# Moving the row loads of VectorE's modulation sums from SyncE's queue to GpSimd's

## The chip, the cores and the metric

The kernel runs on one core of a Trainium2 chip. Its time is the device time of one execution in microseconds (us), and a kernel's time is the median over its runs. The engines are TensorE (PE, matmuls), VectorE (DVE), ScalarE (ACT), GpSimd (POOL) and SyncE (SP). Each works through its own list of instructions in order. A transfer (DMA) is an instruction on the list of the engine that issues it: here SP for most loads, POOL for some stores and loads. An instruction that has to wait holds up all that stand behind it on its engine.

## The reference, cut to what matters

One decoder layer on 512 tokens of width 2048, in float32. A vector `mod` of 6 x 2048 numbers, computed from the conditioning vector `c`, shifts, scales and gates the two halves of the layer.

```python
mod = jax.nn.silu(c) @ w_ada + b_ada
sh1, sc1, gt1, sh2, sc2, gt2 = jnp.split(mod, 6, axis=-1)
h = rms_norm(x, g_pre_mix) * (1.0 + sc1) + sh1
proj = h @ w_in                       # q, k, v, gates, RG-LRU branches
mix = concat(rms_norm(o_att), rms_norm(o_rnn)) @ w_out
x = x + gt1 * rms_norm(mix, g_post_mix)
h = rms_norm(x, g_pre_mlp) * (1.0 + sc2) + sh2
f = jnp.square(jax.nn.relu(h @ w_ff1)) @ w_ff2
x = x + gt2 * rms_norm(f, g_post_mlp)
```

Four of the six parts of `mod` (gt1, sh2, sc2, gt2; numbers 2, 3, 4 and 5 in the code) are computed in the way that the change touches.

## The kernel before, in words

Matmuls run in about float32 accuracy from split operands: a raw weight is copied by ScalarE into a high part and VectorE subtracts that from the raw weight to get the low part, and three matmuls use the pairs. So each weight costs a load, a ScalarE instruction and a VectorE instruction ("the split", lines 102 and 103) before PE can use it. In the first half of the program weights go through two raw buffers `wr` (loaded in line 84, by SP) into slots `sl`. In the two MLP products raw weights `fr` (line 1294, by SP, three buffers) are summed in pairs (`fs`, lines 1315 to 1318) and split into `fh` and `fl` (lines 1299 and 1300), as a Strassen-like scheme with seven products instead of eight wants.

The four modulation parts are not computed on PE but on VectorE, as dot products. `w_ada` is stored transposed, so that a partition holds one output and the free axis the 2048 inputs. `qdot` loads a piece `md` of 128 outputs x 512 inputs (256 KB, line 217) and multiplies it in one VectorE instruction (line 218, "a dot" below) with the row `ca`, which holds 512 values of silu(c) copied to all partitions (line 216, 256 KB), while the products are summed along the free axis into a column of `dq`. Each part takes 64 dots, 256 in all; after every 16 dots `ca` is loaded anew for the next quarter of the inputs. `ca` has one buffer, so its load waits for the last dot with the old one. `md` goes round in a ring of buffers, and a load waits for the dot that used its buffer: six buffers during attention, six shared with other temporaries (`tmp`) during the output projection, and two in the second MLP product.

The program runs in stages: the first projection; attention and RG-LRU with the rest of the input projection (about 217 to 660 us), with 112 dots; the output projection with `wout` (about 660 to 845 us), with 80 dots; the first MLP product; the second (from about 1500 us), with 64 dots from 1478 us on, one at each of its first steps. The output projection goes over four blocks (0 to 3) of 512 columns and 16 pieces of the inner dimension. In blocks 0 to 2, each weight piece serves four row blocks at once; in block 3 the row blocks go one after the other, so that the first of them needs all 16 pieces within a short time. A block is evacuated in line 1072.

The code is written in one order, but a scheduler sets the order in which each engine's list is built, from its own picture of when things are ready; so a change of one queue can move instructions on all engines. POOL's list before holds the stores of the two halves' outputs (`oat`, line 793, and `orn`, line 850), of `ud` (the first MLP product's results, lines 1148, 1421 and 1423) and the loads of `ud` back into `uf` (line 1434), each of which waits for the VectorE work that makes its data or frees its buffer.

Of the kernel before, what the change touches and what calls it, by code (L numbers as in the profile page):

```python
# [13 lines left out]
S = 512  # L14
# [116 lines left out]
def hybrid_block_kernel(ctx: ExitStack, tc: tile.TileContext, xT, c, vec, wada, wst, win, wv0, wv1,  # L131
                        w1, w2, pe, wrg, wout, wff1, wff2, xN, out):
    nc = tc.nc
    V, A, T, G = nc.vector, nc.scalar, nc.tensor, nc.gpsimd
# [73 lines left out]
    def qdot(pool, s_, n, ring=("md", NMD)):  # L208
        for _ in range(min(n, len(QD[s_]))):
            k, q_ = QD[s_].pop(0)  # L210
            w = pool.tile([128, S], F32, name="md", tag=ring[0], bufs=ring[1])
            if k == 0 or CA["pool"] is not pool:
                CA["pool"] = pool
                ca = CA[0] = pool.tile([128, S], F32, name="ca", tag="ca", bufs=1)
                row = cad[0, S * q_:S * q_ + S]
                nc.sync.dma_start(ca, bass.AP(tensor=row.tensor, offset=row.offset, ap=[[0, 128], [1, S]]))
            nc.sync.dma_start(w, wada[s_, k, :, S * q_:S * q_ + S])
            (V.scalar_tensor_tensor(w, w, 0.5, CA[0], op0=OP.mult, op1=OP.mult,  # L218
                                                            accum_out=dq[s_][:, q_, k:k + 1]))

# [726 lines left out]
    def attention(pair, natoms):  # L947
# [10 lines left out]
        for s_ in range(-1, n + TD + 2):  # L958
# [31 lines left out]
            while nmod[0] >= 1:  # L990
                qdot(bp, 2 if QD[2] else 4 if QD[4] else 3, 1)
                nmod[0] -= 1
# [7 lines left out]
    fill(n2 - n1)  # L1000
    attention(1, n3 - n2)
    qdot(bp, 2, 64)
    qvec(gg1, 2, V_GQM)

# [116 lines left out]
    def cdots(x):  # L1121
        nd_[0] += x * nd_[1]
        while nd_[0] >= 1:
            nd_[0] -= 1
            qdot(mp, 4 if QD[4] else 3, 1, ("tmp", NTMP))
# [414 lines left out]
    for s, (kind, q, g) in enumerate(GR):  # L1540
        if kind == "f":
            k, n = q
# [184 lines left out]
```

## Time and profile before

| what | value |
|---|---|
| median of 3 runs | 2205.11 us (2202.41 to 2206.97) |
| profiled execution | 2201.8 us, its span 2200.1 us |
| PE busy | 2095.3 us |
| VectorE busy | 1880.2 us |
| ScalarE busy | 1392.3 us |
| GpSimd busy, its DMA issues counted | 63.7 us |
| VectorE idle just before a dot, waiting for `md` / for `ca` | 34.9 us / 18.5 us |

The span is the time from the first to the last instruction of one profiled execution; the rest of its time lies around it. Busy times are those of the instructions on an engine. A wait is put down to the instruction or transfer that came last before the waiting instruction went on.

### The profile page before, as it was taken

Reading aid. Unit: us, or ns where it says so; the run is one execution under the profiler, and the core shown is the slowest. Engines: PE = TensorE matmul, PEld = TensorE weight load, DVE = VectorE, ACT = ScalarE, POOL = GpSimd, SP = SyncE. Lnnn points to the kernel's source line nnn. Section 1 sums busy time; section 2 is a strip of 40 time slices with the busy share of each in tenths; the row PEclk is TensorE's granted clock in tenths of the full one; section 3 lists DMA queues with packets and bytes.
Section 4 is the critical chain, followed back from the end, with each engine's and each line's share of the span. In section 5 each row is a group of like instructions: output and inputs, shape, how many; then the busy total and the mean of one; then the engine's idle time right before and its main releaser. Section 6 shows DMA issues by size and latency. Waiting matters only on the chain.

```text
span 2200.1 us, 39399 instructions
## 1 busy us (share of the span) xinstructions
PE 2095.3 (95%) x14621; PEld 1915.6 (87%) x14621; DVE 1880.2 (85%) x3762; ACT 1392.3 (63%) x2536; POOL 63.7 (3%) x119
## 2 busy tenths in 40 slices
PE   7998999999999989899999999998999999999995
PEld 3687777878877867899999999998999999999995
DVE  8987999877887777879999999999998887887788
ACT  4349889548994327765555555545766677767764
POOL 0000000000000000000000000000000000000010
PEclk8999999999999999999999999999999999999998
DMA  9764554662126885555555555566766544444453
GB/s 367 310 241 136 191 166 148 219 196 67 59 94 226 285 292 186 192 172 173 186 180 171 176 187 178 192 206 206 253 219 207 190 162 142 165 150 158 138 171 116
DMA packets 138818, 411.12 MB, mean 187 GB/s; under 512 B 18225, under 2 KB 25281, under 8 KB 134273
## 3 DMA queue, kind: packets, MB, share of 16 engines
q1 hardware_dynamic: 126178, 341.49, 46.3%
q0 software_dynamic: 12448, 67.12, 8.8%
q8 instruction: 115, 1.88, 0.3%
q14 instruction: 77, 0.63, 0.1%
HBM read 366.58 MB, written 41.97 MB: 186 GB/s over the span
## 4 chain that ended last, share of the span: by engine, by line
PE 63%; DVE 17%; ACT 8%; DMA 8%; issue 4%; SPq 0%; DVEq 0%; ACTq 0%; POOLq 0%; POOL 0%
DMA md<-wada 4%; PE ps_pj L1132 3%; PE ps_pj L1133 3%; PE ps_pj L1134 3%; DVE fl L1300 3%; PE ps_pj L1479 3%; PE ps_pj L1480 3%; PE ps_pj L1481 3%; DVE md L218 2%; PE ps_S L1134 2%; PE ps_S L1132 2%; PE ps_T L1132 2%; PE ps_S L1133 2%; PE ps_T L1133 2%; PE ps_T L1134 2%
## 5 line engine op out<-in xcount | busy, mean ns | idle before, releaser
L1299 ACT ACTIVATE fh<-fs 128x1024 fp32r<-128x1024 f32 x256 | 273.0, 1066 | 326.2 <-DVE fs L1318 120.9
L1300 DVE TENSOR_TENSOR fl<-fs,fh 128x1024 fp32r<-128x1024 f32 x256 | 312.6, 1221 | 97.1 <-ACT fh L1299 94.6
L1299 ACT ACTIVATE fh<-fr 128x768 fp32r<-128x768 f32 (+2 forms) x296 | 217.1, 735 | 71.5 <-PE ps_pj L1133 11.7
L1300 DVE TENSOR_TENSOR fl<-fr,fh 128x768 fp32r<-128x768 f32 (+2 forms) x296 | 241.1, 816 | 19.1 <-ACT fh L1299 19.0
L102 ACT ACTIVATE sl<-wr 128x512 fp32r<-128x512 f32 (+2 forms) x252 | 145.6, 606 | 146.5 <-DMA wr<-wout 85.2
L218 DVE SCALAR_TENSOR_TENSOR md<-md,ca 128x512 f32<-128x512 f32 x256 | 171.8, 687 | 57.2 <-DMA md<-wada 34.9
L103 DVE TENSOR_TENSOR sl<-wr,sl 128x512 fp32r<-128x512 f32 (+2 forms) x252 | 163.8, 664 | 49.2 <-ACT sl L102 35.9
L1315 DVE TENSOR_TENSOR fs<-fr 128x512 f32<-128x512 f32 x256 | 175.5, 686 | 5.6 <-DMA fr<-wff 3.9
L1479 PE MATMUL ps_pj<-fh,AH 128*128 128x256 f32 x602 | 168.9, 281 | 0.6 <-ACT ps_pj L1459 0.3
L1480 PE MATMUL ps_pj<-fl,AH 128*128 128x256 f32 x602 | 169.0, 281 | 0.0
L1481 PE MATMUL ps_pj<-fh,AL 128*128 128x256 f32 x602 | 168.7, 280 | 0.0
L177 PE MATMUL ps_pj<-AH,sl 128*128 128x512 f32 x384 | 162.2, 422 | 0.4 <-ACT tr L818 0.4
L179 PE MATMUL ps_pj<-AH,sl 128*128 128x512 f32 x384 | 153.5, 400 | 1.5 <-DVE sl L103 1.5
L178 PE MATMUL ps_pj<-AL,sl 128*128 128x512 f32 x384 | 153.5, 400 | 0.0
L1479 PEld LDWEIGHTS ps_pj<-fh,AH 128*128 128x128 f32 x602 | 113.8, 189 | 1.6 <-ACT ps_pj L1459 1.6
L1480 PEld LDWEIGHTS ps_pj<-fl,AH 128*128 128x128 f32 x602 | 113.9, 189 | 0.3 <-DVE fl L1300 0.3
L1481 PEld LDWEIGHTS ps_pj<-fh,AL 128*128 128x128 f32 x602 | 114.0, 189 | 0.0
L1480 PE MATMUL ps_S<-fl,AH 128*128 128x256 f32 x394 | 110.4, 280 | 1.4 <-DVE fl L1300 1.4
L1479 PE MATMUL ps_S<-fh,AH 128*128 128x256 f32 x394 | 110.4, 280 | 1.3 <-ACT ps_S L1459 1.2
L1481 PE MATMUL ps_T<-fh,AL 128*128 128x256 f32 x396 | 110.8, 280 | 0.0
L1479 PE MATMUL ps_T<-fh,AH 128*128 128x256 f32 x396 | 110.8, 280 | 0.0
L1318 DVE TENSOR_TENSOR fs<-fs,fr 128x256 f32<-128x256 f32 x256 | 107.8, 421 | 3.5
(630 smaller groups left out, 7292.7 us busy)
## 6 DMA issues: line engine op xcount, KB each, us to landing
fr<-wff SPq DMA_DIRECT2D x276, 512.0 KB, 3.7
md<-wada SPq DMA_DIRECT2D x256, 256.0 KB, 4.3
uf<-ud POOLq DMA_DIRECT2D x32, 896.0 KB, 4.8
wr<-win SPq DMA_DIRECT2D x48, 512.0 KB, 3.7
ada<-wada SPq DMA_DIRECT2D x22, 1024.0 KB, 10.6
wr<-wout SPq DMA_DIRECT2D x36, 512.0 KB, 4.9
ud<-uf POOLq DMA_DIRECT2D x18, 896.0 KB, 5.3
ud<-uf POOLq DMA_DIRECT2D x14, 768.0 KB, 4.9
```

The lines of the kernel that those rows point to most:

```text
L103: self.nc.vector.tensor_sub(lo, raw, self.f(hi))
L177: T.matmul(o, wh, mh, start=start, stop=False)
L218: (V.scalar_tensor_tensor(w, w, 0.5, CA[0], op0=OP.mult, op1=OP.mult, accum_out=dq[s_][:, q_, k:k + 1]))
L1132: T.matmul(o, wh, b[0], start=start, stop=False, skip_group_check=True)
L1133: T.matmul(o, wh, b[1], start=False, stop=False, skip_group_check=True)
L1134: T.matmul(o, wl, b[0], start=False, stop=stop, skip_group_check=True)
L1299: A.activation(hi, src, AF.Copy)
L1300: V.tensor_sub(lo, src, f(hi))
L1315: V.tensor_add(v2(Sm[:, :512]), v2(R[:, 256:768]), R[:, None, :256].to_broadcast([128, 2, 256]))
L1479: T.matmul(o, uh, hi, start=first and k < 4 and t_ == 0, stop=False, skip_group_check=True)
L1480: T.matmul(o, uh, lo, start=False, stop=False, skip_group_check=True)
L1481: T.matmul(o, ul, hi, start=False, stop=last, skip_group_check=True)
```

## The change

The two transfers of `qdot` are issued from POOL (`G` is `nc.gpsimd`) instead of SP:

```diff
                 CA["pool"] = pool
                 ca = CA[0] = pool.tile([128, S], F32, name="ca", tag="ca", bufs=1)
                 row = cad[0, S * q_:S * q_ + S]
-                nc.sync.dma_start(ca, bass.AP(tensor=row.tensor, offset=row.offset, ap=[[0, 128], [1, S]]))
-            nc.sync.dma_start(w, wada[s_, k, :, S * q_:S * q_ + S])
+                G.dma_start(ca, bass.AP(tensor=row.tensor, offset=row.offset, ap=[[0, 128], [1, S]]))
+            G.dma_start(w, wada[s_, k, :, S * q_:S * q_ + S])
             (V.scalar_tensor_tensor(w, w, 0.5, CA[0], op0=OP.mult, op1=OP.mult,
                                                             accum_out=dq[s_][:, q_, k:k + 1]))
```

On SP, in the output projection, the list before has the loads of weights and of pieces in turn (a row is a line, an operation, what is written and read, its shape, and how many follow each other):

```order
195 L84 DMA wr<-wout 128x1024
196 L217 DMA md<-wada 128x512 x2
197 L216 DMA ca<-cad 128x512
198 L217 DMA md<-wada 128x512 x2
199 L84 DMA wr<-wout 128x1024
200 L217 DMA md<-wada 128x512 x3
201 L1079 DMA xin<-xN 128x512 x2
202 L84 DMA wr<-wout 128x1024
203 L217 DMA md<-wada 128x512 x3
204 L84 DMA wr<-wout 128x1024 x2
```

The same stage on SP with the change:

```order
103 L84 DMA wr<-wout 128x1024
104 L1079 DMA xin<-xN 128x512 x4
105 L84 DMA wr<-wout 128x1024 x21
106 L84 DMA wr<-wff 128x512 x2
107 L1088 DMA x1d<-M 128x512 x4
```

The weights now follow one another, and the loads of `xin` stand ahead of them.

On VectorE, at the end of block 2 of the output projection (its evacuation is line 1072), the list before reads:

```order
1401 L218 SCALAR_TENSOR_TENSOR md,dq_92<-md,ca 128x512 x4
1402 L103 TENSOR_TENSOR sl<-wr,sl 128x512
1403 L218 SCALAR_TENSOR_TENSOR md,dq_92<-md,ca 128x512 x3
1404 L1072 TENSOR_TENSOR M<-ps_pj,gbc 128x512 x2
1405 L1072 TENSOR_TENSOR M<-ps_S,gbc 128x512 x2
1406 L103 TENSOR_TENSOR sl<-wr,sl 128x512 x2
1407 L218 SCALAR_TENSOR_TENSOR md,dq_92<-md,ca 128x512
1408 L103 TENSOR_TENSOR sl<-wr,sl 128x512
1409 L218 SCALAR_TENSOR_TENSOR md,dq_92<-md,ca 128x512 x2
1410 L103 TENSOR_TENSOR sl<-wr,sl 128x512 x3
```

The same place with the change:

```order
1396 L103 TENSOR_TENSOR sl<-wr,sl 128x512 x2
1397 L218 SCALAR_TENSOR_TENSOR md,dq_92<-md,ca 128x512 x7
1398 L103 TENSOR_TENSOR sl<-wr,sl 128x512 x4
1399 L1072 TENSOR_TENSOR M<-ps_pj,gbc 128x512 x2
1400 L1072 TENSOR_TENSOR M<-ps_S,gbc 128x512
1401 L103 TENSOR_TENSOR sl<-wr,sl 128x512
1402 L1072 TENSOR_TENSOR M<-ps_S,gbc 128x512
1403 L218 SCALAR_TENSOR_TENSOR md,dq_92<-md,ca 128x512 x9
1404 L223 TENSOR_TENSOR dq_92<-dq_92 128x32
```

Splits for block 3 (line 103) that stood behind the evacuation stand ahead of it, and the last nine dots of the part stand behind it in one run. Counted from the start of the program, 227 of the 236 splits up to the end of the stage's dots stand ahead of the first row of that evacuation before, and 235 with the change; the dots of the stage ahead of it are 71 of 80 in both.

On VectorE in the second MLP product, around the 40th of its 64 dots, the list before reads:

```order
2535 L218 SCALAR_TENSOR_TENSOR md,dq_94<-md,ca 128x512
2536 L1318 TENSOR_TENSOR fs<-fs,fr 128x256
2537 L218 SCALAR_TENSOR_TENSOR md,dq_94<-md,ca 128x512
2538 L1300 TENSOR_TENSOR fl_18093<-fs,fh_18092 128x1024
2539 L1315 TENSOR_TENSOR fs<-fr 128x512
2540 L1317 TENSOR_TENSOR fs<-fs,fr 128x256
2541 L1318 TENSOR_TENSOR fs<-fs,fr 128x256
2542 L1300 TENSOR_TENSOR fl_18159<-fr,fh_18158 128x768
2543 L218 SCALAR_TENSOR_TENSOR md,dq_94<-md,ca 128x512 x2
2544 L1300 TENSOR_TENSOR fl_18161<-fs,fh_18160 128x1024
```

The same place with the change:

```order
2524 L218 SCALAR_TENSOR_TENSOR md,dq_94<-md,ca 128x512
2525 L1318 TENSOR_TENSOR fs<-fs,fr 128x256
2526 L218 SCALAR_TENSOR_TENSOR md,dq_94<-md,ca 128x512
2527 L1300 TENSOR_TENSOR fl_18093<-fs,fh_18092 128x1024
2528 L1315 TENSOR_TENSOR fs<-fr 128x512
2529 L1317 TENSOR_TENSOR fs<-fs,fr 128x256
2530 L1318 TENSOR_TENSOR fs<-fs,fr 128x256
2531 L218 SCALAR_TENSOR_TENSOR md,dq_94<-md,ca 128x512
2532 L1300 TENSOR_TENSOR fl_18159<-fr,fh_18158 128x768
2533 L218 SCALAR_TENSOR_TENSOR md,dq_94<-md,ca 128x512 x3
2534 L1300 TENSOR_TENSOR fl_18161<-fs,fh_18160 128x1024
```

Between the splits `fl_18093` and `fl_18161` of the same weights stand two dots before and four with the change, three of them in a row. Such a row of three stands at four places in this stage with the change and at none before.

## Rows read from the trace of the kernel before

**Rows 1.** The page, part 1: busy us (share of the span), instructions, PE.

```profile
PE 2095.3 (95%) x14621; PEld 1915.6 (87%) x14621; DVE 1880.2 (85%) x3762; ACT 1392.3 (63%) x2536; POOL 63.7 (3%) x119
```

**Rows 2.** Busy time by stage: stretch, length; PE, PEld, DVE, ACT, POOL; clock, DMA, GB/s.

```profile
217.00:500.00 283.00, 270.84 (x1430) 223.61 (x1430) 253.24 (x799) 207.82 (x484) 4.50 (x8) 0.99 0.57 182
...
720.00:800.00 80.00, 80.00 (x344) 64.26 (x343) 60.00 (x156) 20.40 (x45) 0.00 (x0) 1.00 0.87 295
800.00:826.00 26.00, 16.22 (x57) 10.99 (x57) 17.29 (x42) 8.20 (x19) 0.00 (x0) 0.87 0.84 266
...
1460.00:1727.00 267.00, 250.07 (x2063) 246.37 (x2062) 237.42 (x402) 173.14 (x253) 10.12 (x19) 0.99 0.66 219
```

**Rows 3.** Waits of PE, 720 to 840: total us, times, longest.

```profile
PE ps_pj L915 <- ACT sl L102: 5.7, 3, 3.0
PE ps_pj L916 <- DVE sl L103: 4.1, 2, 3.9
```

**Rows 4.** SP's list in order of time, 793 to 822: start, duration.

```profile
794.60 0.93 SPq L217 DMA_DIRECT2D md<-wada  x2
800.30 0.33 SPq L216 DMA_DIRECT2D ca<-cad  x1
...
802.06 0.38 SPq L84 DMA_DIRECT2D wr<-wout  x1
...
805.98 0.38 SPq L84 DMA_DIRECT2D wr<-wout  x1
```

**Rows 5.** Waits of VectorE, 217 to 500.

```profile
DVE md L218 <- DMA md<-wada: 10.7, 12, 2.7
DVE md L218 <- DMA ca<-cad: 5.8, 3, 3.4
DVE md L218 <- issue: 3.3, 1, 3.3
```

**Rows 6.** Waits of VectorE, 1460 to 1727.

```profile
DVE md L218 <- DMA md<-wada: 15.6, 14, 2.4
DVE md L218 <- DMA ca<-cad: 6.2, 3, 2.9
```

**Rows 7.** The longest wait of PE, 1460 to 1727.

```profile
PE ps_T L1480 <- DVE fl L1300: 4.1, 1, 4.1
```

**Rows 8.** VectorE in order of time, 1657 to 1667; in brackets idle before.

```profile
1658.03 0.68 DVE L218 SCALAR_TENSOR_TENSOR md<-md,ca 128x512 f32<-128x512 f32 x1
...
1662.79 0.69 DVE L218 SCALAR_TENSOR_TENSOR md<-md,ca 128x512 f32<-128x512 f32 x1 [2.86 <-DMA ca<-cad]
...
1664.73 0.69 DVE L218 SCALAR_TENSOR_TENSOR md<-md,ca 128x512 f32<-128x512 f32 x1 [1.24 <-DMA md<-wada]
```

**Rows 9.** DMA issues, whole span: queue, count, KB, median us to landing.

```profile
xin<-xN SPq DMA_DIRECT2D x16, 256.0 KB, 4.7
...
x1d<-M SPq DMA_DIRECT2D x16, 256.0 KB, 2.8
...
orn<-y POOLq DMA_DIRECT2D x8, 256.0 KB, 2.4
...
p<-x1d POOLq DMA_DIRECT2D x8, 256.0 KB, 3.5
ud<-ax POOLq DMA_DIRECT2D x14, 128.0 KB, 3.4
uf<-ud SPq DMA_DIRECT2D x14, 128.0 KB, 2.5
```

**Rows 10.** The same for 715 to 830 (first) and 1480 to 1726.

```profile
md<-wada SPq DMA_DIRECT2D x73, 256.0 KB, 5.4
...
uf<-ud POOLq DMA_DIRECT2D x15, 896.0 KB, 4.9
md<-wada SPq DMA_DIRECT2D x50, 256.0 KB, 3.9
```

**Rows 11.** POOL's issues of line 1434: ns least/median/most, first to last start.

```profile
L1434 POOL DMA_DIRECT2D uf<-ud x32: 531/531/536, 1504.7 to 2070.6; - x32
```

## The prediction

> **What bounds the kernel now.** I read the page's first part first: TensorE (PE) is busy for 95% of the span [rows 1], so the kernel ends when its matmuls end, and only time in which PE stands still can be won. Next the busy time by stage [rows 2]: the reader is to see that PE's gaps are not spread evenly. From 720 to 800 us there is none (344 matmuls in 80 us, 0.233 us each). From 800 to 826 there are 57 matmuls, which at that pace are 13.3 us of work in 26 us: 12.7 us are lost, at a mean granted clock of 0.87 where the stage ahead of it shows 1.00. From 217 to 500 PE stands still for 12.2 us and from 1460 to 1727 for 16.9. These are the three stages in which the moved loads run (112, 80 and 64 of the 256 summed pieces), so they are where the change can act.
>
> Who ends PE's waits? From 720 to 840 it is the split of a raw weight, on ScalarE (5.7 us) or on VectorE (4.1), and nothing else [rows 3]. SyncE's queue shows why the weight came late [rows 4]: SP has issued two `md` loads by 795.5 and then nothing until 800.30, when the dot that frees `ca` is over; only behind that, at 802.06, comes the next `wout` load, and the one after at 805.98. Both streams wait in one line.
>
> From 217 to 500 and from 1460 to 1727 PE waits for VectorE's work, and VectorE itself waits for the moved loads: 10.7 + 5.8 + 3.3 = 19.8 us in the first [rows 5], 15.6 + 6.2 = 21.8 us in the second [rows 6]. One place shows how that reaches PE: its longest wait in the last stage, 4.1 us [rows 7], follows two VectorE waits of 2.86 and 1.24 us at 1660 to 1665 [rows 8], for the one `ca` buffer and for an `md` buffer. There the dots stand close together, the ring has two `md` buffers, and SP was not in the way: this is the time of a load, not a queue.
>
> **The change part by part.** 272 loads (256 of `md`, 16 of `ca`) leave SP's queue and join GpSimd's (POOL). No transfer, dot or matmul is added or removed. The builder's order on the engines changes with it, as shown with the change.
>
> *Issuing.* POOL takes 0.53 us for a load [rows 11]; 272 of them are 144 us spread over 1500, on an engine with nothing else on the path. I cost it at nothing. Behind a waiting `md` load on POOL now stand the stores of `oat`, `orn` and `ud` and the loads of `ud`. In the new order each such store or load waits for VectorE work that stands ahead of the dot which frees the next `md` buffer, so neither holds the other up by more than an issue. If that cover were gone, a late `ud` load would hold VectorE up for its landing, 4.9 us [rows 10].
>
> *Out-projection, 720 to 840.* With the `md` loads gone, SP has 21 `wout` loads in a row, each held only by its own buffer. VectorE's order follows: before, 227 of the 236 splits it does up to there stand ahead of the evacuation of block 2, so 9 of the 16 that block 3 needs come after it, at the very place where PE starves; now 235 do, and 1 comes after. Ahead of it stand the same 71 dots. The 8 splits that move forward cost 8 x 0.62 = 5 us of VectorE earlier, and VectorE has 20 us to spare from 720 to 800 (60.0 busy of 80 [rows 2]). Since its waits for weights go, some of that spare turns into waits for `md`, whose landing is slow in this stage, 5.4 us [rows 10]. Bounds: all 12.7 us come back, or 3 (transfers are already busy for 0.84 to 0.87 of the time there [rows 2]). I take 9, nearer to the full sum, since 8 of the 9 late splits move: **-9 us**.
>
> *Attention, 217 to 500.* The dots stand in nearly the same places. Adding up VectorE's work between each dot and the sixth dot before it (whose buffer it reuses), with 4.2 us for a load, leaves 11 us of waits in either order, nearly all for `ca`, where the trace has 19.8. The other 9 us I put to loads held up behind weights on SP, and they should go. PE stood still for only 12.2 us, so VectorE's gain passes on in part, I estimate a third: **-3 us**, bounds -8 and +2 (a slower landing on POOL).
>
> *Second MLP product, 1460 to 1727.* The same sum over the 64 dots, with the second dot before it (two buffers) and 4.2 us for a load (3.9 to landing in this stage [rows 10] and 0.3 around it), gives 24 us for the order of before, and the trace has 21.8: the sum can be used. The new order has dots packed closer: four places with three in a row, where before there were at most two. The third of three must wait for a load that was issued when the first ended, 4.2 less the one dot between, 3.5 us. The sum for the new order is 30 us, so VectorE is 6 us later than before. VectorE is booked here (237.4 of 267 us busy and 21.8 waiting [rows 2, 6]), and PE shows that such bunches pass through, so I take all of it: **+6 us**. This hangs on the landing: with 3.6 us the new order gives 23 us (about 1 to 2 better than before), with 4.7 it gives 38 (13 worse).
>
> *Landing on POOL's queue.* The trace has no load of `md` there, so I take pairs of like size [rows 9]: 256 KB stores land in 2.4 us from POOL and 2.8 from SP; 256 KB loads in 3.5 from POOL (`p<-x1d`) and 4.7 from SP (`xin`); 128 KB in 3.4 from POOL against 2.5 from SP. So between 1.2 us faster and 0.9 slower; I take no difference, which is what most of these pairs come to.
>
> Sum: -9 - 3 + 6 = -6 us. The profiled execution took 2201.8 us (span 2200.1 and 1.7 around it), so 2195.8 by its own time. It lies 3.3 us below the median of the runs, 2205.1, and the median is what will be measured against: 2205.1 - 6 = **2199 us**.
>
> One rule speaks against any gain. The row first: SP does not run out of issuing time, since a 512 KB weight issue took 0.38 us at 802.06, but it had stood for 4.8 us until 800.30 in front of a load that had to wait [rows 4]. By the Trainium skill, "DMA: Bandwidth & Descriptors", section "Issuing engines are not separate DMA queues", starting transfers from several engines saves only the sequencer's time for starting them; by that the sum would be 0 and the time 2205. The trace agrees that starting costs little (0.33 to 0.38 us), but the gap at 800.30 is a wait of one stream in front of another, which that sentence does not cover.
>
> **The rivals.** *No change.* The weights at 802 to 822 come no sooner, because the transfers themselves are the limit there (0.84 busy, 266 GB/s [rows 2]) and the two raw buffers come free only when VectorE has split them. For it: `wout` loads on this stage are slow to land even when issued promptly. Against it: the stage just ahead moves 295 GB/s. Then the out-projection gives 0, and -3 and +6 leave 2208 us, chance 0.12.
>
> *Slower.* A load from POOL lands later by 0.5 us; the packed dots of the last stage then cost 13 us instead of 6, attention gives nothing back, and the out-projection gives 6: +7, 2212 us. It decides from a landing about 0.25 us longer on. For it: the 128 KB pair [rows 9], POOL's longer issue (0.53 against 0.33 us [rows 11, 4]). Against it: the 256 KB pairs. Chance 0.20.
>
> *More than forecast.* `md` loads no longer stand behind 512 KB weights in the same line and land 0.6 us sooner: the last stage is even, attention gives 6 and the out-projection 12: 2187 us. For it: the x1d pair. Chance 0.14.
>
> *VectorE holds POOL up.* If each VectorE instruction could stop POOL from starting a load, a load would come 0.7 us later (one dot's length [rows 8]): the last stage +16, attention +3, the out-projection -6, so 2218 us. Against it stand POOL's issues from 1504 to 2070, 531 to 536 ns all 32 times [rows 11], in stages where VectorE is busy for 0.8 to 0.9 of the time. Chance 0.04. The Trainium skill, "SBUF — State Buffer", section "SBUF: two separate sides", states such a lock for VectorE's two-port modes and transfers issued from GpSimd; by that rule this rival would be the outcome, and the trace of before shows no sign of it.
>
> **How the numbers follow.** The forecast has 0.50 and a range of its own of 2193 to 2205. What a measurement of this kernel can tell from no change is about 0.2%, 4.4 us. Faster: 0.36 of the forecast's 0.50, and the case of 0.14, 0.50. Same: 0.14 of the forecast and 0.09 of no change, 0.23. Slower: 0.20 + 0.04 and 0.03 of no change, 0.27. The range reaches into the cases on both sides, to half of the larger gain and a little over half of the slower case: 2186 to 2213 leaves out about 0.07 of the one, 0.08 of the other and the 0.04.
>
> **What would show it.** Right: PE's waits for weight splits from 720 to 840 fall from 9.8 us to 3 or less; SP's `wout` loads stand without `md` between them; the VectorE waits of 217 to 500 fall from 20 to about 11 us; in the last stage they rise from 22 to about 28, in a few places of 3 to 5 us; `md` lands in 3.9 to 4.4 us there. Wrong: a landing beyond 4.5 us in the last stage turns the sum over; PE starving at the start of block 3 as before means that the queue was not the reason; long POOL issues mean the lock.

## The result and the profile after

The changed kernel takes **2254.95 us** (median of 4 runs, 2251.95 to 2257.13), the kernel before 2203.76 in the same comparison: a ratio of 1.0235, 95% interval 1.022 to 1.0251. It is 51 us slower, where 6 us of gain were forecast and 8 of loss were the end of the range.

The page's first row of the changed kernel (as [rows 1]), and the busy times by stage (as [rows 2], with 74 us added after 826):

```profile
PE 2110.3 (94%) x14621; PEld 1924.6 (85%) x14621; DVE 1880.6 (83%) x3762; ACT 1393.2 (62%) x2536; POOL 209.6 (9%) x391
```

```profile
217.00:500.00 283.00, 261.94 (x1365) 216.23 (x1365) 241.46 (x758) 195.91 (x454) 68.07 (x127) 0.97 0.55 181
720.00:800.00 80.00, 80.00 (x345) 64.16 (x344) 48.68 (x118) 21.91 (x46) 20.82 (x39) 1.00 0.74 251
800.00:826.00 26.00, 18.96 (x83) 14.90 (x81) 15.91 (x44) 4.61 (x8) 10.66 (x21) 0.95 0.80 279
826.00:900.00 74.00, 57.43 (x225) 42.05 (x226) 49.31 (x125) 32.66 (x83) 10.36 (x20) 0.77 0.62 204
1460.00:1727.00 267.00, 243.63 (x1991) 239.90 (x1990) 229.94 (x396) 159.62 (x234) 40.08 (x75) 0.97 0.64 212
```

VectorE does the same work (1880 us) and POOL has 146 us more, the forecast's 144 us of issues. The transfers' busy share (the last figure but one) is lower in each stretch of [rows 2] than it was; only in the one added behind 826 is it higher, 0.62 where the kernel before has 0.55. What grew is standing still, in all three stages with dots. PE's first and last matmuls of a line (the view of one line) give each stage's length:

```profile
L915 PE MATMUL ps_pj<-sl,AH x128: 388/396/796, 676.0 to 896.8; 128*128 128x512 f32 x128
```

The output projection (L915) starts at 676.0 instead of 662.9 us and lasts 220.8 us from its first to its last start instead of 199.2. The second MLP product (L1479) lasts 673.9 us instead of 651.0. So attention lost 13 us, the output projection 22 and the last stage 23, and the first MLP product between them, which has hardly any moved load, took 2 us less. These three figures are given for every run below, as "stages +13 / +22 / +23". They come from one profile each and scatter: one kernel profiled twice differed by 3.6 us in one stage, and a stage left unchanged read +4.0. Part of the loss is PE's granted clock: 1.00 from 720 to 800 us and, behind the stops, from 826 to 900, a mean of 0.77 between its two levels (1.2 and 2.4 GHz), where the kernel before shows 1.00; a matmul there takes 0.255 us of busy time, against 0.232 from 720 to 800.

VectorE's waits ahead of dots answer to [rows 5, 6]; the windows are 217 to 500, 720 to 880 and 1460 to 1790:

```profile
DVE md L218 <- DMA md<-wada: 18.8, 18, 1.9
DVE md L218 <- DMA ca<-cad: 14.1, 5, 6.6
...
DVE md L218 <- DMA md<-wada: 24.1, 21, 6.6
DVE md L218 <- DMA ca<-cad: 18.1, 4, 6.0
...
DVE md L218 <- DMA md<-wada: 32.4, 20, 4.0
DVE md L218 <- DMA ca<-cad: 2.6, 2, 2.2
```

That is 32.9, 42.2 and 35.0 us, 110 in all where there were 57. PE's waits from 720 to 880, which answer to [rows 3], show what they do in the output projection:

```profile
PE ps_pj L916 <- DVE sl L103: 19.9, 6, 7.4
PE ps_pj L915 <- ACT sl L102: 2.5, 1, 2.5
```

The weights now wait on VectorE instead of SP: a split stands behind dots that wait for their loads.

One reload of `ca` shows a load's turn, from the end of the dot that frees the buffer to the next dot. VectorE, then POOL, of the changed kernel:

```profile
785.15 0.69 DVE L218 SCALAR_TENSOR_TENSOR md<-md,ca 128x512 f32<-128x512 f32 x1
791.92 0.69 DVE L218 SCALAR_TENSOR_TENSOR md<-md,ca 128x512 f32<-128x512 f32 x1 [4.86 <-DMA ca<-cad]
```

```profile
786.15 0.54 POOL L216 DMA_DIRECT2D ca<-cad  x1 [4.49 <-DVE md L218]
793.53 3.26 POOL L217 DMA_DIRECT2D md<-wada  x6 [6.84 <-DVE md L218]
```

The dot ends at 785.84, the issue starts 0.31 us later and takes 0.54, and the next dot starts 6.1 us after the last one. At 793.53 six `md` loads take POOL 3.26 us to issue. Over the whole run a load lands in 4.5 us by the median and 14.1 at most (`md`; 4.3 and 7.5 before). A landing is counted from the start of the issue, so it holds the longer issue.

### The profile page after: what moved, and what is told of

The parts are those of the page before. It is cut to its first block, busy times and chain, and to the rows that moved or that the text cites. A ratio compares the mean times of both kernels' runs of the same rounds, so it can differ in the third digit from the quotient of the medians.

```text
span 2255.4 us, 39453 instructions
## 1 busy us (share of the span) xinstructions
PE 2110.3 (94%) x14621; PEld 1924.6 (85%) x14621; DVE 1880.6 (83%) x3762; ACT 1393.2 (62%) x2536; POOL 209.6 (9%) x391
## 4 chain that ended last, share of the span: by engine, by line
PE 56%; issue 17%; DVE 10%; DMA 7%; ACT 6%; POOL 4%; POOLq 0%; SPq 0%; DVEq 0%; ACTq 0%
POOL md L217 4%; PE ps_pj L1132 3%; PE ps_pj L1133 3%; PE ps_pj L1134 3%; DMA md<-wada 3%; PE ps_pj L1479 2%; PE ps_pj L1480 2%; PE ps_T L1132 2%; PE ps_pj L1481 2%; PE ps_T L1133 2%; PE ps_T L1134 2%; PE ps_S L1134 2%; PE ps_S L1132 2%; PE ps_S L1133 2%; PE ps_S L1479 1%
## 5 line engine op out<-in xcount | busy, mean ns | idle before, releaser
L217 POOL DMA_DIRECT2D md<-wada x256 | 137.5, 538 | 403.8 <-DVE md L218 307.2
L1479 PE MATMUL ps_pj<-fh,AH 128*128 128x256 f32 x602 | 169.4, 282 | 1.4 <-ACT ps_pj L1459 1.3
L1480 PE MATMUL ps_T<-fl,AH 128*128 128x256 f32 x396 | 111.3, 281 | 6.0 <-DVE fl L1300 6.0
L1479 PEld LDWEIGHTS ps_pj<-fh,AH 128*128 128x128 f32 x602 | 114.2, 190 | 2.6 <-ACT ps_pj L1459 2.6
L1479 PE MATMUL ps_S<-fh,AH 128*128 128x256 f32 x394 | 110.9, 281 | 1.3 <-ACT ps_S L1459 1.2
```

Source lines behind the costliest of these rows:

```text
L217: G.dma_start(w, wada[s_, k, :, S * q_:S * q_ + S])
L1479: T.matmul(o, uh, hi, start=first and k < 4 and t_ == 0, stop=False, skip_group_check=True)
L1480: T.matmul(o, uh, lo, start=False, stop=False, skip_group_check=True)
```

## The experiments

Each run was timed against the kernel before on the same chip. One word is needed first. To **pin** an order means that the builder is told that each instruction of an engine stands behind the one given before it; that is an order, not a wait, and no instruction is added:

```python
for a, b in zip(names, names[1:]):
    tc.add_manual_dep(at[b], a, NoSync)
```

The names are listed in the order of VectorE, ScalarE and PE in the kernel before, or in the changed one. SP's and POOL's lists are then made by the builder around it. In the other diffs, E stands for the queue. No run leaves out or changes any computation.

### Queue and order apart

```diff
-            nc.sync.dma_start(w, ...)   # ca alike
+            G.dma_start(w, ...)
+        pin(order of before)
```

> All moved loads are issued from POOL as in the changed kernel, but VectorE, ScalarE and PE keep, instruction by instruction, the order that they had before the change. Theory Q (the queue): a load issued from POOL comes back later, because a freed buffer is followed by an issue 0.26 us later and 0.2 us longer, and a ca load lands about 1 us later; the order counts for little. Then this takes about 2245 to 2255 us, with 90 to 110 us of VectorE's waits ahead of dots. Theory O (the order): what costs is the new order on VectorE, with up to 15 dots in a row and the weight splits behind them. Then this takes about 2204 (2196 to 2210), with waits ahead of dots near 53 us as before. My own estimate from the loops of the trace: attention by the queue (+10), output projection mostly by the order (+3 here), second MLP product half and half (+10): about 2227.

Measured (e1): 2237.0 us, ratio 1.0170 (1.0156 to 1.0183), stages +11 / +16 / +6. The queue alone costs 36 us, with one reserve: pinning alone, with all loads on SP, was not run. The run e5 below, which pins and moves only `ca`, costs 7 us in all; unless the move of `ca` gained something, pinning costs no more. One other thing differs on SP: two loads of `xin` stand earlier there, and issue without a wait. VectorE's waits in the three windows are 31.5, 27.5 and 32.4 us.

```diff
+        pin(order of the changed kernel)   # loads stay on SP
```

> The loads stay on SP as before, but VectorE, ScalarE and PE take, instruction by instruction, the order of the changed kernel. Theory Q: about 2204 us. Theory O: about 2255 us. My own estimate, the complement of the run before: attention +3, output projection +18, second MLP product +10, about 2235.

Measured (e2): 2237.3 us, 1.0162 (1.0146 to 1.0178), stages +7 / +23 / +14. The order, with the list that the builder made for SP around it, costs 36 us too, and the two together 51, so they overlap. Neither theory holds alone. In the output projection this run is not clean: around the new order the builder put up to 14 `md` loads in a row ahead of a weight on SP, and ScalarE, which waits for the weights, stood for up to 15.7 us (11.5 at most in the kernel before). SP's list, then the wait from 662 to 900:

```profile
817.49 11.47 SPq L217 DMA_DIRECT2D md<-wada  x14
830.67 0.33 SPq L216 DMA_DIRECT2D ca<-cad  x1
831.04 0.90 SPq L217 DMA_DIRECT2D md<-wada  x2
832.04 0.85 SPq L84 DMA_DIRECT2D wr<-wout  x2
```

```profile
ACT sl L102 <- DMA wr<-wout: 111.7, 23, 15.7
```

### One stage at a time

```diff
+            E = G if ring[0] == "tmp" else nc.sync      # e3; e4: ring == ("md", 2)
```

> Only the 80 loads of md and 5 of ca of the output projection are issued from POOL; attention and the second MLP product keep SP. If the three stages' losses are independent, as the position of PE's matmuls in time suggests (the changed kernel is 13.1 us late at 801 us of before and 34.6 us late at 862), this costs that stage's 21 us alone: 2225 us. If the loss there came from being late out of attention, or from POOL's list being full of earlier loads, it costs less than 8 us: below 2212.

> Only the 64 md and 4 ca loads of the second MLP product are issued from POOL. Independent stages: the 22 us that the changed kernel lost between 1584 and 2120 us of before, so 2226 us. If the late arrival of that stage in the changed kernel was needed for the loss: under 2212. The prediction's step for this stage, +6, would give 2210.

Measured: e3 2218.3 us, 1.0085 (1.0069 to 1.0101), stages +4 / +19 / 0; e4 2220.2 us, 1.0092 (1.0078 to 1.0106), stages +3 / +4 / +17. Each stage loses by itself; no stage needs the lateness of another. The builder's order moved with each, inside the stage that was changed.

### Which loads, with the old order

e5 issues only `ca` from POOL, e6 only `md`; both are pinned to the order of before.

> As the run with POOL and the old order, but only the 16 loads of ca are issued from POOL; the 256 of md stay on SP. In the run with all loads on POOL and the old order, VectorE waited 14.8 us longer for ca and 17.3 us longer for md than before (33.3 and 52.2 against 18.5 and 34.9). Theory C (the ca loads carry about half of the queue's cost by themselves): waits for ca near 33 us, for md near 35, time about 2216 us. Theory M (ca comes late only because six md loads are then also in flight from POOL ahead of it): waits for ca stay near 19 us, time about 2201 to 2205 us.

> The reverse: the 256 loads of md from POOL, the 16 of ca from SP, order of before on VectorE, ScalarE and PE. Theory C: waits for md near 52 us, for ca near 19, time about 2220 us. Theory M: nearly the whole of the 36 us that POOL costs with the old order, 2230 us or more, unless ca is helped by standing on the other queue, and then about 2220 too; the run with ca alone decides between the two.

Measured: `ca` alone (e5) 2207.9 us, 1.0032 (1.0021 to 1.0044); `md` alone (e6) 2232.6 us, 1.0145 (1.0131 to 1.0159), stages +9 / +18 / +6. Nearly all of the queue's cost is that of `md`; neither theory gave the 7 us of `ca`. Idle time of VectorE ahead of dots, in us and times, with `md` alone on POOL:

```profile
  DMA md<-wada: 49.5, 42
  DMA ca<-cad: 44.7, 14
```

The waits for `ca` are the longest of all runs, with `ca` on SP. SP starts these issues 0.04 us after the dot and takes 0.33, as before. So it is not the issue that makes a `ca` late here but its landing (4.1, 5.0 and 7.5 us in the output projection, 4.9 to 5.9 in attention); what is under way beside it is the likely reason, and no run shows it.

### More buffers in the last stage

```diff
-                qdot(OPP["p"], 5, 1, ("md", 2))
+                qdot(OPP["p"], 5, 1, ("md", 3))
```

> The kernel before, with three md buffers instead of two in the second MLP product. If the time of a load (3.9 us) against the distance of the dots in the ring is what makes VectorE wait 22 us in that stage, the waits for md fall from 15.6 to under 6 us and PE gains 8 to 12 us there: about 2190 to 2194 us. Rival: PE's waits there come from the other VectorE work (237 of 267 us busy), and the time stays within 4 us of 2202.

> The changed kernel, with three md buffers instead of two in the second MLP product. If the later return of a load through two buffers is what cost 22 us in that stage, most of it goes: about 2235 to 2240 us, with the two other stages as they were. Rival: the order of VectorE's other work in that stage, which moved too, costs it: then 2248 or more.

Measured: on SP (e7) 2202.0 us, 1.0006 (0.9995 to 1.0016); in the changed kernel (e8) 2237.0 us, 1.0163 (1.0149 to 1.0178), stages +14 / +19 / +6. In the changed kernel a third buffer takes away some 16 of the 51 us (by the two ratios). This run is not pinned, and more than the turn through two buffers changed in it, as shown below. On SP the waits for `md` fell to 6.5 us too, and the time did not. VectorE from 1460 to 1790 in that run:

```profile
DVE fs L1315 <- DMA fr<-wff: 9.6, 2, 8.9
DVE md L218 <- DMA md<-wada: 6.5, 7, 1.8
```

Behind the last dot the finished part `gg` is stored to `ggd` (line 1601), and the load of `gbc` from `ggd` (line 1013) waits until that store has landed. Both stand on SP, with weights `fr` behind them: here SP stands from 1685.2 to 1695.3, and VectorE then waits 8.9 us for `fr`. What the dots gave, a weight took back.

The same pair costs the changed kernel. SP, VectorE and PE there, then SP's wait:

```profile
1764.68 0.38 SPq L1601 DMA_DIRECT2D ggd<-gg  x1
1777.73 0.33 SPq L1013 DMA_DIRECT2D gbc<-ggd  x1
...
1786.31 0.69 DVE L1315 TENSOR_TENSOR fs<-fr 128x512 f32<-128x512 f32 x1 [11.04 <-DMA fr<-wff]
...
1788.65 0.58 PE L1480 MATMUL ps_O<-fl,AH 128*128 128x256 f32 x1 [7.66 <-DVE fl L1300]
...
SPq L1013 <- DMA ggd<-gg: 12.5, 1, 12.5
```

In the kernel before, SP stands nearly as long, but VectorE waits only 2.4 us:

```profile
1734.12 0.38 SPq L1601 DMA_DIRECT2D ggd<-gg  x1
1745.70 0.33 SPq L1013 DMA_DIRECT2D gbc<-ggd  x1
...
1752.06 0.69 DVE L1315 TENSOR_TENSOR fs<-fr 128x512 f32<-128x512 f32 x1 [2.36 <-DMA fr<-wff]
```

The difference is the place: in the changed kernel the pair stands four weight loads earlier in SP's list, as it does in e2 and e4. PE stands for 7.7 us by it, the longest stop of that stage, and for 4.5 and 4.6 us in those two; in the kernel before, in e1 and in e8 it has no such stop of over 1 us. So up to 7.7 of the 16 us may be this stop, and the turn's own share is not shown.

### One line or two

e9 issues every transfer that SP had from POOL, e10 only the raw weights (lines 84 and 1294); both are pinned to the order of before.

> All transfers that SP issued, weights too, are issued from POOL, in one line again; VectorE, ScalarE and PE keep the order of before. Theory P (POOL's own path: an issue starts 0.26 us later after a buffer comes free and takes 0.54 instead of 0.33 us): md and ca pay what they paid with the old order and the weights pay as well, so 2232 us or more. Theory L (two lines: md and ca now share the transfer engines with weights that used to be issued behind them): with one line there is nothing to share, waits ahead of dots stay near 55 to 65 us, and the time is 2204 to 2214 us.

> The two lines the other way round: md and ca stay on SP, the raw weights (wr and fr) are issued from POOL; VectorE, ScalarE and PE keep the order of before. Theory P: md and ca are as before and no longer stand behind weights, whose buffers are ahead of need: 2195 to 2206 us. Theory L: two lines again, ca lands in 5 to 7 us in the output projection as it did in the two other splits, and the time is 2220 to 2235 us.

Measured: everything on POOL (e9) 2248.1 us, 1.0222 (1.0204 to 1.0240), stages +17 / +11 / +3; the weights on POOL (e10) 2235.7 us, 1.0164 (1.0147 to 1.0181). Theory L falls with the first: one line again, and it is slower still. The second was expected to tell the same and doesn't, since the text overlooked that weights have a ring too, of two raw buffers, and pay POOL's turn in it: the start of the output projection is 19 us late, 10 of them before the first dot. So these weights, too, lose by going through a short ring from POOL. In the output projection 11 of the 16 us of e1 stay with one line, in e9; the other 5 are little more than the scatter. The three stages of e9 add up to 31 of its 48 us lost; the first MLP product, whose weights come from POOL there too, lost another 11.

### A longer turn on SP

```diff
-            nc.sync.dma_start(w, wada[s_, k, :, ...])
+            nc.sync.dma_start(w[:64], wada[s_, k, :64, ...]); nc.sync.dma_start(w[64:], wada[s_, k, 64:, ...])
+        pin(order of before)
```

> All loads on SP, order of before on VectorE, ScalarE and PE, but each md is loaded as two halves of 64 partitions, so that its second half is issued about 0.33 us later. Theory T (the turn of a load is what costs; a sum over the distances of the dots in the trace of before gives 16 us more waiting per us of turn in attention, 7 to 9 in the output projection and 14 to 16 in the last stage): 0.33 us more is some 13 us of waits and 2208 to 2220 us. Rival: a queue on SP hides it, since halves move faster and POOL's cost is its own: within 4 us of 2201.

Measured (e13): 2268.5 us, 1.0307 (1.0289 to 1.0324), stages +26 / +38 / +7, the slowest of all, without POOL. The sign is theory T's and the size is not. In part that is because the added time was not 0.33 us. The `md` issues on SP, least/median/most in ns:

```profile
L217 SPq DMA_DIRECT2D md<-wada x512: 465/587/1867, 216.0 to 1785.3; - x171
```

A half takes 0.59 us to issue, longer than a whole load (0.33): SP spends 300 us on `md` instead of 84, and each second half starts 0.6 us late. By the theory's own sum over the distances that explains some 33 us (an estimate) of the 68; VectorE's waits ahead of dots rose by 55, from 57 to 112. That the rest is bursts of loads, each standing behind the issues of those ahead of it, is argued and not shown.

### Dots with room between them

On VectorE, dots are moved back behind instructions that follow them, until each stands a load's turn behind the dot whose buffer it uses; ScalarE and PE keep the order of before. The piece from the last stage, before and after:

```order
 L1317 TENSOR_TENSOR fs<-fs,fr 128x256
-L218 SCALAR_TENSOR_TENSOR md,dq_94<-md,ca 128x512
-L1318 TENSOR_TENSOR fs<-fs,fr 128x256
-L218 SCALAR_TENSOR_TENSOR md,dq_94<-md,ca 128x512
+L1318 TENSOR_TENSOR fs<-fs,fr 128x256
 L1300 TENSOR_TENSOR fl_16890<-fs,fh_16889 128x1024
+L218 SCALAR_TENSOR_TENSOR md,dq_94<-md,ca 128x512 x2
```

> Loads on SP as before; ScalarE and PE keep the order of before; on VectorE 119 dots are moved back behind one or more of the instructions that follow them (up to 28 in attention, up to 6 in the two other stages), so that each stands at least a load's turn (4.15 us in attention, 5.5 in the output projection, 4.1 in the last stage) behind the dot whose buffer it uses. Theory S (spacing: what costs is the turn of a load against the distance of the dots that share its buffer, and PE pays for VectorE's waits): waits ahead of dots fall from 57 us to about 17 to 25, and the time to 2180 to 2192 us. Rival: PE's stops come from the weights and not from the dots; then waits fall and the time stays within 4 us of 2201.

> The same with all moved loads on POOL, and 138 dots moved back for turns of 4.8, 5.9 and 5.0 us. Theory S: with room between the dots POOL's longer turn is hidden, waits ahead of dots fall from 91 us (POOL, old order) to 25 to 35, and the time from 2237 to 2190 to 2203 us. Rival (POOL's line costs in another way, by transfers that collide with the weights or by the weights' own turns): 2215 us or more.

Measured: on SP (e11) 2200.5 us, 1.0001 (0.9991 to 1.0010), stages 0 / +13 / -6; on POOL (e12) 2215.1 us, 1.0070 (1.0057 to 1.0083), stages 0 / +20 / -2. The waits ahead of dots fell to 27 and 29 us, the first a little above what was expected and the second as expected, and with them went all of POOL's loss in attention and in the last stage. The times came 8 and 12 us above the ranges expected, that on POOL where the rival had it: the output projection ate the gain. There no dot was moved past an evacuation, with whose temporaries it shares the `tmp` buffers, so the dots piled up ahead of one, and PE stood (PE from 815 to 832, SP kernel):

```profile
827.39 0.80 PE L916 MATMUL ps_pj<-sl,AH 128*128 128x512 f32 x1 [19.37 <-DVE sl L103]
```

VectorE's own list between 806.9 and 824.3 is 17 dots in a row (the expectations below say 20). The split that PE wants stands behind them. This is the cost of a run of dots in its purest form. A second profile of the SP kernel (2199.4 us) shows a stop of the same kind in the same place.

So the spacing was left out of that stage; the old order is kept there:

> Loads on SP, dots spaced in attention and in the last stage only (76 dots moved back), the output projection in the order of before. In the two runs with all stages spaced, PE won 2 us in attention and 5 us in the last stage against the kernel before and lost 9 to 13 us in the output projection behind a bunch of 20 dots. If that bunch was the reason, this takes 2192 to 2196 us and beats both kernels; if PE's gains were noise of single profiles, 2198 to 2203.

> The same with all moved loads on POOL (95 dots moved back, for turns of 4.8 and 5.0 us). Of POOL's 36 us with the old order, the 12 of attention and the 6 of the last stage should be gone and the last stage's gain of 5 be there, and the 12 to 16 us of the output projection should stay: 2206 to 2214 us. If POOL's line costs in those stages by something that room between the dots does not cover: 2220 us or more.

> As the run before it (POOL, dots spaced in attention and in the last stage, the same order on VectorE, ScalarE and PE), but the 85 moved loads of the output projection are issued from SP again; POOL keeps the 187 of the two spaced stages. If room between the dots covers POOL's longer turn there, this is as fast as the spaced kernel with SP, 2188 to 2196 us, and the queue costs nothing in these stages. If POOL's cost is only shifted, 2202 us or more.

Measured: with SP (e15) **2190.6 us**, ratio 0.9950 (0.9937 to 0.9963), stages -2 / +1 / -5, which beats both kernels. With POOL (e16) 2215.8 us, 1.0060 (1.0046 to 1.0075), stages +1 / +19 / -2. With POOL in the two spaced stages alone and the order of e16 (e17) 2198.7 us, 0.9994 (0.9985 to 1.0003), stages -1 / -1 / +3. So 15 to 17 (by ratios or medians) of the 25 us between the first two lie in the output projection, the one stage where the dots had no room. The orders of the two kernels differ a little as well: with SP, 76 dots were moved back, with POOL 95. The last run fell between its two expectations: with POOL in two stages it is no slower than the kernel before, and 8 to 10 us slower than SP with spaced dots, most of that in the last stage (+3 against -5). VectorE's waits ahead of dots in the run that beats both, 217 to 500 and 1460 to 1790:

```profile
DVE md L218 <- DMA md<-wada: 1.6, 2, 1.1
DVE md L218 <- DMA ca<-cad: 0.7, 1, 0.7
...
DVE md L218 <- DMA md<-wada: 6.2, 5, 2.0
DVE md L218 <- DMA ca<-cad: 0.6, 1, 0.6
```

From 42 us ([rows 5, 6]) to 9. PE won 7 us of them.

## Why the prediction was wrong

**Out-projection, -9: the step that failed.** It was the largest term and had the wrong sign: a gain of 9 us was forecast and the stage lost 22. The prediction counted the splits ahead of block 2's evacuation (235 instead of 227) and took more splits ahead for earlier splits. It did not ask what stands ahead of each split: the same 71 dots, in fewer and longer runs (the stage's 80 dots stand in 24 runs instead of 32, the last two of 7 and 9). It said that VectorE had 20 us to spare and that "some of that spare turns into waits"; all of it did and more, since the waits in that stage rose by 29 us, from 13 to 42. And it is the old order that kept weights and loads in step: SP's one line, read as the fault in [rows 4], let a weight through after each few loads. The rows of the order shown with the change had the runs of 7 and 9 in them; the sum by distances that was made for the two other stages was not made here. Made afterwards with 4.7 us a turn, it gives 12.7 us of waits for the old order and 22.8 for the new (15.6 and 20.5 when summed again from the two traces). What it leaves of the measured 42 is open, as said below.

**Issuing, costed at nothing: failed.** The 144 us were right as a size and wrong as free. POOL starts 0.31 us after the dot, SP 0.04; it issues in 0.54 us, SP in 0.33 (the lines are in the sections on the result and on the hardware). That is half a microsecond on each load that a dot is waiting for. The forecast looked for other work on POOL that could be held up and found none, rightly; the work held up was the load itself.

**Attention, -3: failed.** Its sum used a ring of six buffers. The text ahead of the prediction says so as well, and it is not so: the ring there is `("md", NMD)`, and NMD is 4. With four, the same sum gives 22.6 us at 4.2 us a turn for the order of before and 23.6 for the new one, against 19.8 in the trace: the turn explains the whole wait, and nothing was left for "loads held up behind weights". Summed again from the two traces it comes out 2 to 3 us lower in both orders, so the order makes no difference either way. With 4.7 us it gives 30 and 31; the runs show 32.9 for the change and 31.5 for POOL with the old order. Waits rose where the prediction has them falling from 20 to 11.

**Last stage, +6: the mechanism held in part, the size did not.** VectorE's waits rose from 21.8 to 35.0 us and the stage lost 23. The order alone costs 14, the queue alone 6, and a third buffer takes back 17. The packed dots and the short ring are one part of it, and the prediction's sum had to be taken at POOL's turn instead of 4.2 us. The step from 24 to 30 us that it gave to the packing alone doesn't come out again: summed from the two traces, with each wait putting off all that follows, 4.2 us give 18.4 for the order of before and 21.4 for the new, and 4.7 give 26.0 and 28.2. The other part is outside the sum: the store of `ggd` came earlier in SP's list, the weights behind it came late, and PE stood for 7.7 us at once. Its sign to look for, a landing beyond 4.5 us, did not come (4.0 by the median in that stage), because the added time lies ahead of the end of the issue: from there to the landing the two queues take alike, some 4.0 us each by the medians of the run.

**Landing, no difference: held for `md` by the median, not in the tail.** 4.5 against 4.3 us over the run. For `ca` it did not hold in the output projection, where the median went from 4.2 to 5.7 us. And the first `md` loads of the output projection came in bursts beside other loads and took up to 14.1 us.

**The rivals.** "Slower, 2212" was the right kind, a later load through packed dots, with a turning point of 0.25 us that the added 0.48 us passed; it priced that for the last stage only. "No change" and "more gain" fell. VectorE's lock did not show: all 256 issues of `md` took 537 to 547 ns. The forecast went too far in saying that by that lock this rival would be the outcome: the lock that it names is one of two-port modes, and no row shows VectorE in one here. The rule of the Trainium skill by which the sum would be 0 ("DMA: Bandwidth & Descriptors", section "Issuing engines are not separate DMA queues") agrees in that no transfer rate was won, 182 against 187 GB/s over the span; its sum of 0 does not, since the queue alone cost 36 us, and the measurement decides. The same page of the Trainium skill, in its section "Specifications", gives about 1 us to a first byte from GpSimd and about 0.6 from SyncE and ScalarE. The 0.48 us here is near that difference of 0.4, though no trace shows a first byte, and the forecast had not weighed it.

**What stays open.** In the output projection the queue costs 16 to 19 us with the old order, more than half a microsecond times the loads there that a dot waits for. Part of it may be that loads in two lines share the transfer engines (`ca` took 5.5 to 6.8 us to land in three of four reloads there, 3.2 to 4.9 before); no run separates that from the turn, and e6 only shows that a `ca` on SP is late too when `md` is on POOL. With `ca` on POOL and `md` on SP (e5) they take 6.4, 4.3, 5.3 and 5.6 us there, with that stage back on SP (e17) 3.0 to 5.1. In the last stage, what the earlier place of the `ggd` store costs was not run by itself.

## What to carry to other kernels

Where a load waits for the buffer of an earlier use, and a later use stands waiting for that load, its price is the whole turn, from the freeing instruction through the issue to the landing, set against the work between the two uses; a queue that starts and issues half a microsecond later is paid at each such load. Read the buffer counts from the calls, sum that turn for every stage, and on an engine that works in order look at what stands behind each waiting instruction. Look also for a store and a load of the same data next to each other on one queue, since all that stands behind them waits for the store to land. Room between the uses was worth more here than another queue: moving 76 dots back behind instructions that followed them gave 0.5%, and with 95 moved back POOL's loss in those two stages shrank to some 2 us, within the scatter.

## What the runs showed of the hardware that was not expected

- From the end of a freeing dot to the start of the next issue: 0.31 us on POOL, 0.04 on SP, in nearly all reloads of `ca` in all runs (on SP one stood longer behind other loads); the issue itself 0.54 and 0.33 us. For SP, the dot and the `ca` load of the run with the new order:

```profile
811.20 0.69 DVE L218 SCALAR_TENSOR_TENSOR md<-md,ca 128x512 f32<-128x512 f32 x1
```

```profile
811.93 0.33 SPq L216 DMA_DIRECT2D ca<-cad  x1
```

- On SP a load of 64 partitions takes longer to issue (0.59 us) than one of 128 (0.33).
- One `ca` issue on POOL starts 2.9 us after the dot that it waits for, as the 114th transfer that POOL issues, in six kernels (the changed one, e1, e8, e12, e16 and e17), where the other reloads take 0.3; with everything on POOL (e9) it is the 210th, and 2.9 us too. What it waits for the profile does not show:

```profile
460.57 0.55 POOL L216 DMA_DIRECT2D ca<-cad  x1 [2.71 <-issue]
```
